# w_ple and the per-layer input brought and turned during the last product of the FFN, and its transposes one token ahead of its products

## The chip, the cores and the metric

One core of a Trainium2 chip runs the whole program. The metric is the device time of one execution in microseconds (us); the time of a kernel is the median of several runs. Engines are called TensorE (PE in the rows, its weight loads PEld), VectorE (DVE), ScalarE (ACT), GpSimd (POOL) and SyncE (SP, whose queue SPq issues most of the DMAs).

## The reference

The program computes one decoder layer for 1024 tokens of 1024 channels: two token mixers, a gated FFN, and at the end a gated per-layer input embedding, which is where the change lies. With `h` the sum after the mixers and `f` the FFN's inner activations (1024 tokens x 2816):

```
f = (gelu(f_gate) * f_val) @ w_down              # 2816 -> 1024
h = h + rmsnorm(f, norm_ffn_post)
e = (p @ w_ple) * sigmoid(h @ w_ple_gate)        # p: 1024 tokens x 256, w_ple: 256 x 1024
h = h + rmsnorm(e, norm_ple_post)                # the output
```

All is float32. A product in that precision is made of three matmuls (`mm3`, lines 342 to 347): each operand is split into a high part (a rounded copy, made by ScalarE) and a low part (the operand less the high part, made by VectorE or GpSimd), and high x high, high x low and low x high are summed in PSUM.

## The kernel before

**The down projection.** `down` (line 1426) makes `f @ w_down` by a scheme of seven block products in place of eight. The sums of activation blocks were written to DRAM before (`acts`), and four weight tiles `b11`, `b12`, `b21`, `b22` of 128 x 11 x 512 hold the blocks of w_down or differences of them. `product` (line 1446) is the loop of one block product: for each of 11 slices j, a pair of slices of `acts` is loaded into `araw` by SyncE every second j (a tag with two buffers); ScalarE makes the high halves of the activations (`whl`) and of the weights (`wdhl`, three buffers in the pool `wdT`); VectorE makes the low half of `whl`, GpSimd that of `wdhl` (all at line 313); TensorE makes 12 matmuls of 128 x 512 into four banks.

The last two products stand in `ple` (line 1504). The first of them, here called **P3**, multiplies the activations 5 with `b12`, which by then holds a difference of weights called **T3** here; the second, **P4**, multiplies the activations 2 with `b21`. Both tiles lie in the pool `wdB`. During P3 the eight blocks of w_ple_gate are loaded and split (`resident`, line 1300). During P4, at every third j, `res` (line 1515) closes one token block of the FFN: it squares it on ScalarE, and VectorE multiplies it with the norm's weights (line 1524) and adds the residual `h1r` (line 1527), with a small power on GpSimd between.

**The embedding.** After P4, `des.close()` gives up the pools of the weight tiles, and a pool `pleA` opens in their place. w_ple is loaded in two blocks of 128 x 1024 and split, the first low half on VectorE, the second on GpSimd. For each of eight blocks of 128 tokens, called tokens here, `inp` (line 1549) loads 128 x 256 of p, turns it by two transposes on TensorE and splits it while copying it out of PSUM (`to_T`, line 368: `ph` on ScalarE, `pl` on VectorE), and makes 12 matmuls into `pi`, which ScalarE copies to `pe` (four buffers). `turn` turns the finished h by eight transposes (`hh`, `hl`), and `out` makes the 48 matmuls of the gate (`pg`), the sigmoid, the norm and the store. The loop's round t makes turn(t+1), inp(t+3), res(t+4) and out(t); inp(0) to inp(2) stand ahead of it, so rounds 0 to 4 hold an input and rounds 5 to 7 none.

**What sets the order.** Buffers and waits are put in by the framework. The order on each engine is written ahead of time by a planner: it simulates the program with costs of its own, and each engine takes, of the instructions that are ready in the simulation, the one that stands first in the program. On the chip each engine then runs its list in that order, and an instruction that isn't ready holds up those behind it. `behind(a, b)` (line 1334) makes what is written in its block stand behind instruction a on a's engine and behind b on b's: `self.araw` is the last load of activations (SyncE), `up.lo` the last low half of activations (VectorE). It makes no wait.

Of the kernel before, what the change touches and what calls it, by code (L numbers as in the profile page):

```python
# [7 lines left out]
F32 = mybir.dt.float32  # L8
F32R = mybir.dt.float32r
# [6 lines left out]
P = 128  # L16
SEQ = 1024
NT = SEQ // P
DM = 1024
KD = DM // P  # L20
# [9 lines left out]
NF = DFF // P  # L30
# [264 lines left out]
class Body:  # L295
# [1130 lines left out]
    def down(self, hes, psd, bank, h1d, up):  # L1426

        nc, io = self.nc, self.io
        hf = NF // 2
        acts, wdn, pre = up.acts, up.wdn, up.pre  # L1430
        wes, des = ExitStack(), ExitStack()
        facc = self.pool(hes, "facc", side="right", own=True).tile([P, NT, DM], F32, name="facc")
        wA = self.pool(wes, "wdA", own=True)
        wB = self.pool(des, "wdB", side="right", own=True)
        thp = self.pool(des, "wdT", side="right", own=True)
        quad = {}
        for key, pool in (((0, 0), wA), ("T2", wA), ((1, 1), wA), ((1, 0), wB), ((0, 1), wB)):
            quad[key] = pool.tile([P, hf, 512], F32, name=f"wd{key[0]}{key[1]}")
        b11, b12, b21, b22, t2 = quad[0, 0], quad[0, 1], quad[1, 0], quad[1, 1], quad["T2"]

        def load_w(k, c, j0, j1):
            r = (k * hf + j0) * P
            nc.sync.dma_start(quad[k, c][:, j0:j1], wdn[r:r + (j1 - j0) * P, c * 512:c * 512 + 512].rearrange(
                "(j p) n -> p j n", p=P))

        def product(src, B, banks, first):

            for j in range(hf):
                if j % 2 == 0:
                    raw = self.wp.tile([P, 2, 512], F32, name="araw", tag="raw", bufs=2)  # L1450
                    m = min(2, hf - j)
                    self.araw = nc.sync.dma_start(raw[:, 0:m], acts[src, j:j + m].rearrange("j p n -> p j n")).ins
                a = up.ring(raw[:, j % 2], nc.vector)
                w = thp.tile([P, 2, 512], F32R, name="wdhl", tag="wdhl", bufs=3)
                self.wlo = self.hl(w[:, 0], w[:, 1], B(j) if callable(B) else B[:, j], nc.gpsimd)
                for t in range(4):
                    s = slice(t * P, t * P + P)
                    self.mm3(banks[t], a[:, 0, s], a[:, 1, s], w[:, 0], w[:, 1], first and j == 0, j == hf - 1,
                             not first)
                yield j  # L1460

        def run(gen, loads=()):

            loads = dict(loads)
            for j in gen:
                with self.behind(self.araw):
                    for ld in loads.get(j, ()):
                        load_w(*ld)

        c0, c1 = slice(0, 512), slice(512, DM)  # L1470
        npre = 2 * len(pre)
        Q = [bank("dq") for _ in range(4)]

        run(product(0, lambda j: pre[j // 2][:, j % 2] if j < npre else b11[:, j], Q, True),
            ((0, ((0, 0, npre, 8), (0, 0, 8, hf))), (2, ((1, 0, 0, 4),)), (4, ((1, 0, 4, 8),)), (6, ((1, 0, 8, hf),)),
             (8, ((1, 1, 0, 4),))))
        for t in range(4):
            nc.scalar.activation(facc[:, t, c0], Q[t], AF.Copy)
        M = [bank("dm") for _ in range(4)]
        run(product(1, b21, M, True), ((0, ((1, 1, 4, 8),)), (2, ((1, 1, 8, hf),)), (4, ((0, 1, 0, 4),)),  # L1480
                                       (6, ((0, 1, 4, 8),)), (8, ((0, 1, 8, hf),))))
        for t in range(4):
            nc.vector.tensor_add(facc[:, t, c0], M[t], facc[:, t, c0])
        Z = [bank("dz") for _ in range(4)]
        for j in product(6, b22, Z, True):
            with self.behind(up.lo):
                nc.vector.tensor_sub(b11[:, j], b12[:, j], pre[j // 2][:, j % 2] if j < npre else b11[:, j])
                nc.vector.tensor_sub(t2[:, j], b22[:, j], b11[:, j])
        for t in range(4):
            nc.scalar.activation(facc[:, t, c1], Z[t], AF.Copy)  # L1490
        for j in product(4, t2, Q, False):
            with self.behind(up.lo):
                nc.vector.tensor_sub(b12[:, j], b22[:, j], b12[:, j])
                nc.vector.tensor_sub(b21[:, j], b21[:, j], t2[:, j])
        for t in range(4):
            nc.scalar.activation(facc[:, 4 + t, c0], Q[t], AF.Copy)
        run(product(3, b11, Q, False))
        for t in range(4):
            nc.vector.tensor_add(facc[:, t, c1], Q[t], facc[:, t, c1])
            nc.scalar.activation(facc[:, 4 + t, c1], Q[t], AF.Copy)  # L1500
        wes.close()
        self.ple(hes, up, product, b12, b21, des, facc, psd, bank, h1d)

    def ple(self, hes, up, product, b12, b21, des, facc, psd, bank, h1d):

        nc, io = self.nc, self.io
        es = ExitStack()
# [5 lines left out]
        c0, c1 = slice(0, 512), slice(512, DM)  # L1513

        def res(t):

            h1 = [self.wq.tile([P, 512], F32, name="h1r", tag=f"s{t % 2 * 2 + i + 1}") for i in range(2)]
            for i, c in enumerate((c0, c1)):
                nc.sync.dma_start(h1[i], h1d[t, :, c])
            jk = self.wq.tile([P, DM], mybir.dt.bfloat16, name="jk", tag="p1", bufs=2)  # L1520
            f = facc[:, t]
            ss = self.small.tile([P, 1], F32, name="ss_h2", tag="ss", bufs=3)
            nc.scalar.activation(jk, f, AF.Square, accum_out=ss)
            nc.vector.tensor_mul(f, f, wf)
            r = self.rstd_of(ss, 1, 1.0 / DM, "h2")
            for i, c in enumerate((c0, c1)):
                nc.vector.scalar_tensor_tensor(f[:, c], f[:, c], r, h1[i], ALU.mult, ALU.add)

        N = [[bank("dn") for _ in range(4)] for _ in range(2)]
# [5 lines left out]
        for t in range(4):  # L1535
            nc.vector.tensor_add(facc[:, 4 + t, c1], N[0][t], facc[:, 4 + t, c1])
            nc.vector.tensor_add(facc[:, 4 + t, c0], N[0][t], facc[:, 4 + t, c0])
        for j in product(2, b21, N[1], True):
            if j % 3 == 0:
                with self.behind(self.araw, up.lo):  # L1540
                    res(j // 3)
        for t in range(4):
            nc.vector.tensor_add(facc[:, 4 + t, c0], N[1][t], facc[:, 4 + t, c0])
        des.close()
        pa = self.pool(es, "pleA", side="right", own=True)
        we = self.resident(pa, "w_ple", range(2))
        pes, hs = {}, {}

        def inp(t):

            pt = self.wp.tile([P, 256], F32, name="pt", tag="hi", bufs=2)
            nc.sync.dma_start(pt, io["p"][0, 0, t * P:t * P + P, :])
            ph = pa.tile([P, 2, P], F32R, name="ph", tag="ph", bufs=2)
            pl = pa.tile([P, 2, P], F32R, name="pl", tag="pl", bufs=2)
            self.to_T(pt, ph, pl, 0, psd, f"p{t}", kt=2, tag="d")
            pe = pes[t] = pa.tile([P, DM], F32, name="pe", tag="pe", bufs=4)
            for hf in range(2):
                c = slice(hf * 512, hf * 512 + 512)
                ps = bank("pi")
                for k, (wh, wl) in enumerate(we):  # L1560
                    self.mm3(ps, ph[:, k], pl[:, k], wh[:, c], wl[:, c], k == 0, k == 1)
                nc.scalar.activation(pe[:, c], ps, AF.Copy)

        def turn(t):
            hh = pa.tile([P, KD, P], F32R, name="hh", tag="hh", bufs=2)
            hl = pa.tile([P, KD, P], F32R, name="hl", tag="hl", bufs=2)
            self.to_T(facc[:, t], hh, hl, 0, psd, f"h{t}", tag="d")
            hs[t] = hh, hl

        def out(t):  # L1570
            hh, hl = hs.pop(t)
# [16 lines left out]
            for hf, c in enumerate(cs if t == NT - 1 else [slice(0, DM)]):  # L1588
                nc.vector.scalar_tensor_tensor(e[:, c], e[:, c], r0[:, 1:2], facc[:, t, c], ALU.mult, ALU.add)
                (nc.scalar, nc.sync)[hf].dma_start(self.out[0, t * P:t * P + P, c], e[:, c])  # L1590

        turn(0)
        for t in range(3):
            inp(t)
        for t in range(NT):
            if t + 1 < NT:
                turn(t + 1)
            if t + 3 < NT:
                inp(t + 3)
            if t + 4 < NT:  # L1600
                res(t + 4)
            out(t)
        es.close()
        hes.close()

# [22 lines left out]
```

## Time and profile before

| | |
|---|---|
| median of three runs | 1985.65 us (1981.07 to 1990.55) |
| the profiled execution's own time | 1987.6 us |
| its span, first to last instruction | 1985.9 us |
| TensorE busy | 1856.9 us (94%) |
| VectorE busy | 1237.1 us (62%) |
| ScalarE busy | 921.9 us (46%) |
| GpSimd busy | 703.1 us (35%) |
| mean granted clock of TensorE | 0.971 |

Busy time of TensorE is that of its matmuls, whose ends are modelled: two that follow each other at full rate overlap in the rows, so the pitch from start to start tells the rate. A wait is shown in brackets behind an instruction, with the instruction that ended it. Times in the rows are us from the span's start; P3 runs to about 1812, P4 from there to 1847, and the rest is the embedding.

### The profile page before, as it was taken

Reading aid. Unit: us, or ns where it says so; the run is one execution under the profiler, and the core shown is the slowest. Engines: PE = TensorE matmul, PEld = TensorE weight load, DVE = VectorE, ACT = ScalarE, POOL = GpSimd, SP = SyncE. Lnnn points to the kernel's source line nnn. Section 1 sums busy time; section 2 is a strip of 40 time slices with the busy share of each in tenths; the row PEclk is TensorE's granted clock in tenths of the full one; section 3 lists DMA queues with packets and bytes.
Section 4 is the critical chain, followed back from the end, with each engine's and each line's share of the span. In section 5 each row is a group of like instructions: output and inputs, shape, how many; then the busy total and the mean of one; then the engine's idle time right before and its main releaser. Section 6 shows DMA issues by size and latency. Waiting matters only on the chain. (4 is left out here: it accounts for less than half of the span.)

```text
span 1985.9 us, 25905 instructions
## 1 busy us (share of the span) xinstructions
PE 1856.9 (94%) x9247; PEld 1535.3 (77%) x9247; DVE 1237.1 (62%) x2364; ACT 921.9 (46%) x1818; POOL 703.1 (35%) x538
## 2 busy tenths in 40 slices
PE   7999989999989999999999959999999999999898
PEld 6788778888778888778777847787787877777776
DVE  5437933341367667776783497776676864958543
ACT  4344222232367667776662334444444544455332
POOL 2132112223122112231162056666666664545100
PEclk9998999999989999999999979999999999999999
DMA  5124333322311010110063212232323356245201
GB/s 163 33 78 116 93 86 90 84 84 80 99 32 33 27 38 29 42 59 22 22 233 129 86 63 91 90 101 85 122 83 109 100 186 239 75 155 173 88 35 43
DMA packets 182943, 178.68 MB, mean 90 GB/s; under 512 B 27869, under 2 KB 133662, under 8 KB 182814
## 3 DMA queue, kind: packets, MB, share of 16 engines
q1 hardware_dynamic: 180592, 170.33, 27.7%
q10 hardware_dynamic: 2222, 6.69, 0.9%
q8 instruction: 73, 1.20, 0.3%
q14 instruction: 56, 0.46, 0.1%
HBM read 132.65 MB, written 44.34 MB: 89 GB/s over the span
## 5 line engine op out<-in xcount | busy, mean ns | idle before, releaser
L345 PE MATMUL pj<-uh,whi 128*128 128x512 f32 x640 | 263.0, 411 | 8.8 <-DVE y L515 6.6
L346 PE MATMUL pj<-ul,whi 128*128 128x512 f32 x640 | 258.4, 404 | 0.0
L347 PE MATMUL pj<-uh,wlo 128*128 128x512 f32 x640 | 258.3, 404 | 0.0
L313 POOL TENSOR_TENSOR wlo<-raw,whi 128x1024 fp32r<-128x1024 f32 x48 | 116.8, 2435 | 323.5 <-ACT whi L324 287.7
L345 PEld LDWEIGHTS pj<-uh,whi 128*128 128x128 f32 x640 | 123.5, 193 | 36.4 <-issue 5.7
L313 POOL TENSOR_TENSOR whl<-s,whl 128x512 fp32r<-128x512 f32 x88 | 126.8, 1448 | 60.2 <-ACT whl L1331 60.2
L347 PEld LDWEIGHTS pj<-uh,wlo 128*128 128x128 f32 x640 | 123.1, 192 | 29.0
L346 PEld LDWEIGHTS pj<-ul,whi 128*128 128x128 f32 x640 | 123.4, 193 | 25.9
L313 POOL TENSOR_TENSOR wdhl<-wd,wdhl 128x512 fp32r<-128x512 f32 x66 | 97.9, 1495 | 78.4 <-ACT wdhl L1331 76.9
L313 POOL TENSOR_TENSOR whl<-raw,whl 128x512 fp32r<-128x512 f32 x66 | 105.4, 1599 | 49.2 <-ACT whl L1331 48.7
L313 DVE TENSOR_TENSOR whl<-araw,whl 128x512 fp32r<-128x512 f32 x77 | 87.1, 1141 | 56.2 <-ACT whl L1331 55.0
L1243 DVE TENSOR_TENSOR Tl<-pt,Th 128x512 fp32r<-128x512 f32 (+1 forms) x152 | 92.6, 617 | 24.9 <-ACT Th L1242 21.2
L345 PE MATMUL q<-mxh,whl 128*128 128x512 f32 x264 | 104.5, 399 | 3.3 <-ACT u L106 2.1
L1213 ACT ACTIVATE Pt<-Pt,nm 128x640 f32<-128x640 f32 (+7 forms) x128 | 93.0, 728 | 30.1 <-DVE nm L1211 29.7
L346 PE MATMUL q<-mxl,whl 128*128 128x512 f32 x264 | 104.2, 395 | 0.0
L347 PE MATMUL q<-mxh,whl 128*128 128x512 f32 x264 | 103.5, 395 | 0.2 <-POOL whl L313 0.2
L1242 ACT ACTIVATE Th<-pt 128x512 fp32r<-128x512 f32 (+1 forms) x152 | 79.2, 538 | 50.0 <-PE po L1246 32.5
L324 ACT ACTIVATE whi<-raw 128x1024 fp32r<-128x1024 f32 x48 | 50.5, 1052 | 83.7 <-PE pj L346 55.8
L1239 PE MATMUL pt<-ident,Pt 128*128 128x128 f32 x528 | 82.9, 277 | 2.8 <-DVE Tl L1243 1.3
L126 DVE SCALAR_TENSOR_TENSOR yg<-c,cv,yg 128x1 f32<-128x1 f32 (+2 forms) x88 | 81.4, 929 | 0.9 <-ACT yg L123 0.9
L1331 ACT ACTIVATE whl<-s 128x512 fp32r<-128x512 f32 x88 | 54.7, 624 | 56.9 <-PE n L347 44.1
L1205 PE MATMUL ps<-kst,qs 128*128 128x512 f32 (+3 forms) x192 | 70.4, 368 | 6.7 <-DVE mx L1208 4.9
(534 smaller groups left out, 5142.0 us busy)
## 6 DMA issues: line engine op xcount, KB each, us to landing
raw<-in_w_up SPq DMA_DIRECT2D x44, 512.0 KB
raw<-in_w_in SPq DMA_DIRECT2D x40, 512.0 KB
araw<-acts SPq DMA_DIRECT2D x35, 512.0 KB
acts<-sd SPq DMA_DIRECT2D x44, 256.0 KB
gates_d<-yz SPq DMA_DIRECT2D x40, 256.0 KB
acts<-yv SPq DMA_DIRECT2D x33, 256.0 KB
gt<-gates_d SPq DMA_DIRECT2D x32, 256.0 KB
wd<-in_w_down SPq DMA_DIRECT2D x7, 1024.0 KB
```

The lines of the kernel that those rows point to most:

```text
L126: self.body.nc.vector.scalar_tensor_tensor(y, src, w, y, ALU.mult, ALU.add)
L313: return eng.tensor_sub(lo, src, hi.bitcast(F32)).ins
L324: nc.scalar.activation(hi, raw, AF.Copy)
L345: nc.tensor.matmul(ps, lh, rh, start=start, stop=False, skip_group_check=more)
L346: nc.tensor.matmul(ps, lh, rl, start=False, stop=False, skip_group_check=more)
L347: nc.tensor.matmul(ps, ll, rh, start=False, stop=stop, skip_group_check=more)
L1205: nc.tensor.matmul(ps[:, 0:n], qs[:, hh], kh, start=True, stop=False)
L1213: nc.scalar.activation(Pt[:, hh, 0:nk], Pt[:, hh, 0:nk], AF.Exp, scale=2.0 ** -(h0 + hh + 1), bias=nm[:, br, hh:hh + 1], accum_out=rs[:, b ...
L1239: nc.tensor.transpose(pt[:, b, hh], Pt[:, hh, (b0 + b) * P:(b0 + b + 1) * P], self.ident)
L1242: nc.scalar.activation(Th[:, 0:m], pt[:, 0:m], AF.Copy)
L1243: nc.vector.tensor_sub(Tl[:, 0:m], pt[:, 0:m], Th[:, 0:m].bitcast(F32))
L1331: self.nc.scalar.activation(hi, src, AF.Copy)
```

## The change

The pool `pleA` goes. The tile of T3 (tag `wd01`) is taken over after P3 as one flat tile `cB`, which holds the four halves of w_ple and two slots of turned input; the tile `b21` (tag `wd10`) is taken over after P4 as `cH`, for the turned h; `pe` takes the three buffers of `wdhl`. Within P4, both blocks of w_ple are loaded and split at j = 1 and 2, both low halves on VectorE; p is loaded in two loads of 512 KB (four tokens each) at j = 4 and 5; tokens 0 and 1 are turned at j = 8 and 10. The raw data go through the two buffers `rawv` that the gate's blocks used in P3. Behind P4, `inp_T` makes the transposes of a token and `inp` its products: round t now makes turn(t+1), inp_T(t+3), inp(t+2), res(t+4), out(t). The work computed is the same.

```diff
-        for j in product(2, b21, N[1], True):
-            if j % 3 == 0:
-                with self.behind(self.araw, up.lo):
-                    res(j // 3)
-        for t in range(4):
-            nc.vector.tensor_add(facc[:, 4 + t, c0], N[1][t], facc[:, 4 + t, c0])
-        des.close()
-        pa = self.pool(es, "pleA", side="right", own=True)
-        we = self.resident(pa, "w_ple", range(2))
-        pes, hs = {}, {}
+
+        flat = lambda tag: wB.tile([P, NF // 2 * 512], F32R, name="ple" + tag, tag=tag)
+        cB = flat("wd01")
+        we, raws, pes, hs = [], [], {}, {}
+        cut = lambda t, i, n, w: t[:, i * n:i * n + n].rearrange("p (k w) -> p k w", w=w)
+
+        def w_ple(k):
+            raw = self.wq.tile([P, DM], F32, name="raw", tag="rawv", bufs=2)
+            nc.sync.dma_start(raw, self.dram2d("w_ple", 2 * P, DM)[k * P:k * P + P, :])
+            w = [cB[:, (2 * k + i) * DM:(2 * k + i + 1) * DM] for i in range(2)]
+            self.hl(*w, raw, nc.vector)
+            we.append(w)
+
+        def p_in(n):
+            raw = self.wq.tile([P, 4, 256], F32, name="pt", tag="rawv", bufs=2)
+            nc.sync.dma_start(raw, io["p"][0, 0, n * 512:n * 512 + 512, :].rearrange("(t p) n -> p t n", p=P))
+            raws.append(raw)
+
+        def inp_T(t):
+
+            o = 4 * DM // 256 + t % 2 * 2
+            self.to_T(raws[t // 4][:, t % 4], cut(cB, o, 256, P), cut(cB, o + 1, 256, P), 0, psd, f"p{t}", kt=2, tag="d")
 
         def inp(t):
 
-            pt = self.wp.tile([P, 256], F32, name="pt", tag="hi", bufs=2)
-            nc.sync.dma_start(pt, io["p"][0, 0, t * P:t * P + P, :])
-            ph = pa.tile([P, 2, P], F32R, name="ph", tag="ph", bufs=2)
-            pl = pa.tile([P, 2, P], F32R, name="pl", tag="pl", bufs=2)
-            self.to_T(pt, ph, pl, 0, psd, f"p{t}", kt=2, tag="d")
-            pe = pes[t] = pa.tile([P, DM], F32, name="pe", tag="pe", bufs=4)
+            o = 4 * DM // 256 + t % 2 * 2
+            ph, pl = cut(cB, o, 256, P), cut(cB, o + 1, 256, P)
+            pe = pes[t] = thp.tile([P, DM], F32, name="pe", tag="wdhl", bufs=3)
...
+        also = {1: (w_ple, 0), 2: (w_ple, 1), 4: (p_in, 0), 5: (p_in, 1), 8: (inp_T, 0), 10: (inp_T, 1)}
+        for j in product(2, b21, N[1], True):
+            with self.behind(self.araw, up.lo):
+                if j % 3 == 0:
+                    res(j // 3)
+                if j in also:
+                    also[j][0](also[j][1])
+        for t in range(4):
+            nc.vector.tensor_add(facc[:, 4 + t, c0], N[1][t], facc[:, 4 + t, c0])
+        cH = flat("wd10")
+
         def turn(t):
-            hh = pa.tile([P, KD, P], F32R, name="hh", tag="hh", bufs=2)
-            hl = pa.tile([P, KD, P], F32R, name="hl", tag="hl", bufs=2)
-            self.to_T(facc[:, t], hh, hl, 0, psd, f"h{t}", tag="d")
-            hs[t] = hh, hl
+            hs[t] = [cut(cH, t % 2 * 2 + i, DM, P) for i in range(2)]
+            self.to_T(facc[:, t], *hs[t], 0, psd, f"h{t}", tag="d")
...
         turn(0)
-        for t in range(3):
-            inp(t)
+        inp(0)
+        inp_T(2)
+        inp(1)
         for t in range(NT):
             if t + 1 < NT:
                 turn(t + 1)
             if t + 3 < NT:
-                inp(t + 3)
+                inp_T(t + 3)
+            if t + 2 < NT:
+                inp(t + 2)
             if t + 4 < NT:
                 res(t + 4)
             out(t)
+        des.close()
         es.close()
```

## Rows read from the trace of the kernel before

**Rows 1.** The page's head.
```profile
span 1985.9 us, 25905 instructions
```

**Rows 2.** Busy time by stretch: length, five engines, granted clock, DMA share, GB/s.
```profile
1812.20:1847.10 34.90, 32.69 (x140) 25.02 (x139) 31.49 (x35) 11.46 (x20) 18.01 (x14) 1.00 0.45 147
1847.10:1861.50 14.40, 10.14 (x45) 7.72 (x44) 9.00 (x12) 6.81 (x14) 3.80 (x2) 0.88 0.25 78
...
1942.50:1954.60 12.10, 12.10 (x59) 9.86 (x58) 5.29 (x9) 3.51 (x8) 0.55 (x1) 1.00 0.11 43
```

**Rows 3.** TensorE's waits, 1780 to 1986: total us, times, longest.
```profile
PE pi L345 <- ACT ph L376: 7.1, 6, 3.3
PE dn L347 <- DVE whl L313: 2.1, 3, 0.9
```

**Rows 4.** Chain of work that ended last, seam behind P4: start, us, what.
```profile
1843.72 5.48 DMA raw<-in_w_ple
...
1849.28 1.06 ACT w_pleh L1310
...
1851.31 0.28 ACT ph L376
```

**Rows 5.** Timeline of TensorE, seam: start, us, what, [idle before <-releaser].
```profile
1846.92 0.49 PE L374 MATMUL pT_h<-ident,facc 128*128 128x128 f32 x3
1847.93 0.44 PE L374 MATMUL pT_p<-ident,pt 128*128 128x128 f32 x2 [0.51 <-DMA pt<-in_p]
1851.64 0.50 PE L345 MATMUL pi<-w_pleh,ph 128*128 128x512 f32 x1 [3.27 <-ACT ph L376]
...
1853.75 0.80 PE L345 MATMUL pi<-w_pleh,ph 128*128 128x512 f32 x1 [0.47 <-ACT ph L376]
...
1855.63 0.62 PE L374 MATMUL pT_p<-ident,pt 128*128 128x128 f32 x2
...
1856.31 0.40 PE L345 MATMUL pi<-w_pleh,ph 128*128 128x512 f32 x1
```

**Rows 6.** Timeline of TensorE, one round of the token loop.
```profile
1877.55 1.03 PE L374 MATMUL pT_h<-ident,facc 128*128 128x128 f32 x8
1878.42 0.38 PE L374 MATMUL pT_p<-ident,pt 128*128 128x128 f32 x2
1879.66 0.50 PE L345 MATMUL pi<-w_pleh,ph 128*128 128x512 f32 x1 [0.85 <-ACT ph L376]
...
1893.77 1.03 PE L374 MATMUL pT_h<-ident,facc 128*128 128x128 f32 x8
```

**Rows 7.** Timeline of TensorE, two slices of P3.
```profile
1806.60 1.10 PE L345 MATMUL dn<-wdhl,whl 128*128 128x512 f32 x4
...
1809.41 1.10 PE L345 MATMUL dn<-wdhl,whl 128*128 128x512 f32 x4
```

**Rows 8.** VectorE's groups by shape, 1781.2 to 1812.2: busy us, mean ns.
```profile
L313 DVE TENSOR_TENSOR w_ple_gatel<-raw,w_ple_gateh 128x1024 fp32r<-128x1024 f32 x7 | 9.6, 1377 | 2.5 <-ACT w_ple_gateh L1310 2.3
```

**Rows 9.** Timeline of VectorE, P3, P4 and the seam.
```profile
1794.56 2.32 DVE L313 TENSOR_TENSOR w_ple_gatel<-raw,w_ple_gateh 128x1024 fp32r<-128x1024 f32 x1
...
1814.99 3.48 DVE L313 TENSOR_TENSOR whl<-araw,whl 128x512 fp32r<-128x512 f32 x2
...
1823.17 0.68 DVE L313 TENSOR_TENSOR whl<-araw,whl 128x512 fp32r<-128x512 f32 x1
...
1842.73 0.68 DVE L313 TENSOR_TENSOR whl<-araw,whl 128x512 fp32r<-128x512 f32 x1
1845.49 2.48 DVE L1543 TENSOR_TENSOR facc<-dn,facc 128x512 f32<-128x512 f32 x4 [2.08 <-PE dn L347]
...
1858.30 0.42 DVE L377 TENSOR_TENSOR pl<-pT_p,ph 128x256 fp32r<-128x256 f32 x1 [2.18 <-ACT ph L376]
```

**Rows 10.** Timeline of SyncE's queue, P4.
```profile
1816.80 7.45 SPq L1452 DMA_DIRECT2D araw<-acts  x2
```

**Rows 11.** Timeline of GpSimd, P4.
```profile
1811.51 6.40 POOL L313 TENSOR_TENSOR wdhl<-wd,wdhl 128x512 fp32r<-128x512 f32 x4
```

More of the change, by code (lines that the diff above doesn't have):

```diff
@@ L1437, in down @@
         for key, pool in (((0, 0), wA), ("T2", wA), ((1, 1), wA), ((1, 0), wB), ((0, 1), wB)):
-            quad[key] = pool.tile([P, hf, 512], F32, name=f"wd{key[0]}{key[1]}")
+            quad[key] = pool.tile([P, hf, 512], F32, name=f"wd{key[0]}{key[1]}", tag=f"wd{key[0]}{key[1]}")
         b11, b12, b21, b22, t2 = quad[0, 0], quad[0, 1], quad[1, 0], quad[1, 1], quad["T2"]
@@ L1501, in down, with ple @@
         wes.close()
-        self.ple(hes, up, product, b12, b21, des, facc, psd, bank, h1d)
-    def ple(self, hes, up, product, b12, b21, des, facc, psd, bank, h1d):
+        self.ple(hes, up, product, b12, b21, des, wB, thp, facc, psd, bank, h1d)
+    def ple(self, hes, up, product, b12, b21, des, wB, thp, facc, psd, bank, h1d):
         nc, io = self.nc, self.io
```

## The prediction

> **What bounds the kernel now.** I read the views in this order: span, busy time by stage, TensorE's waits at the end, the chain of waits, then the order on each engine there. The span is 1985.9 us and TensorE works through nearly all of it [rows 1], so a change is worth what it gives TensorE back where TensorE stands still. The diff touches the part behind about 1805 us: the product P4 (1812.2 to 1847.1), the seam behind it, and eight tokens of the per-layer embedding.
>
> In P4 TensorE is busy 32.69 of 34.90 us, and VectorE 31.49; in the seam, 1847.1 to 1861.5, TensorE works 10.14 of 14.40 us, and the granted clock has a mean of 0.88 [rows 2]. The reader is to see two different causes there. In P4 the waits, 2.1 us in three, are for `whl`, VectorE's low halves; behind P4 they are 7.1 us in six for `ph`, the turned layer input [rows 3]. What ended last in the seam is a load: `w_ple` takes 5.48 us from issue to landing, ScalarE then copies it (1.06), and behind that copy stands ph (0.28) for the first input product [rows 4].
>
> **What the waits cost.** A product matmul is issued every 0.234 us (12 in 2.81 us [rows 7]), a transpose every 0.109 (8 in 0.87 us [rows 6]).
> The seam: from 1846.92, where P4's products have been issued, to 1856.31, where full pitch is back, are 9.39 us [rows 5]. Nine product matmuls and nine transposes lie in it: 9 x 0.234 + 9 x 0.109 = 3.09. Lost: 6.3 us. That is the waits of 0.51, 3.27 and 0.47 [rows 5], about 1.1 us of matmuls at half the rate (the four from 1853.75 to 1855.63 stand 0.47 apart; the lower of the two clock levels, 1.2 GHz, after TensorE had stood), and the restarts.
> The token loop: with an input in it a round takes 16.22 us (1877.55 to 1893.77 [rows 6]). Its work is 48 + 12 products and 8 + 2 transposes, 60 x 0.234 + 10 x 0.109 = 15.13. Lost: 1.09, of which 0.85 is the wait for ph, which comes straight behind the transposes that ph is copied from [rows 6]. There are four such rounds: 4.4 us. A round without an input took 12.10 and has no loss [rows 2] (48 x 0.234 + 0.87 = 12.10), so this is all there is to win in the loop.
> Together 10.7 us.
>
> **The change part by part.**
> *w_ple (two 512 KB loads, two copies, two subtractions) goes into P4.* Its place is the tile of T3, read for the last time in P3, so it need not wait for P4. The cover for the loads is P4's 34.9 us. Gone is the 3.27 us wait; late next at that place is `hh` of token 0 or the bank of the first `pi`, and both are at hand, since turn(0)'s place is the tile that P4's last copy frees. Cost: the copies lie on ScalarE, which is busy only 11.46 us in P4 [rows 2]. The low halves lie on VectorE, which has hardly a gap there: TensorE's three waits in P4 are already waits for VectorE, and what is queued ahead of a `whl` moves TensorE. The nearest rows are the gate's low halves, same shape and engine, mean 1.377 us of seven in P3, and 2.32 for the longest [rows 8, 9]. I take 2 x 1.38 = 2.8 us, all on the path.
> *The input in two loads of 512 KB in the place of eight of 128 KB, queued in P4 behind P4's own loads; two of the eight turnings in P4.* SyncE's queue is in order: `p_in` waits for a buffer that w_ple's low half frees, and behind it stands the next `araw`. In P4 SyncE holds two araw triggers over 7.45 us because the buffers are not free [rows 10], so there is room for p_in if VectorE has finished w_ple by then; I cost it at nothing, and at one exposed load (below) if not. Four transposes move from behind the seam into P4, no gain or loss, with 0.1 us for each of two changes from products to transposes and back. Their two `pl` subtractions (0.42 us each [rows 9]) come late in P4: VectorE's last whl ends at 1843.41 and it then stands 2.08 us [rows 9], which covers 0.84.
> *Transposes one token ahead in the loop.* The matmuls that cover the copy are the previous input's 12 (2.8 us) and the 48 of the gate (11.2 us); a copy of some 0.3 us needs neither in full. Late next would be `pe`: three buffers in place of four, but also made two rounds ahead in place of three, so its slot was and is freed by the token just finished. I cost it at nothing.
> *What stays lost.* 0.1 us at each of five changes between transposes and products, so the gain is 10.7 - 0.5 = 10.2 us, rounded to 10.1.
>
> Sum: 10.1 - 2.8 - 0.2 = 7.1 us less. P4's cost is the uncertain term. Its low end is below nothing: a new order on VectorE can also take away the three waits (-2.1 [rows 3]). Its high end is two low halves of 2.32, two pl and the changes: 4.64 + 0.84 + 0.2 = 5.7. I take 3.0, near the mean of the gate's rows, since these are the same instruction under the same neighbours. The gain is then 12.2 to 4.4.
>
> Whether two subtractions cost their mean or the long form hangs on GpSimd: a `whl` takes 0.68 us at 1823.17, but two take 3.48 from 1814.99 on, while GpSimd makes four `wdhl` in 6.40 [rows 9, 11]. The Trainium skill, "SBUF — State Buffer", section "Who interferes with whom", has a rule that speaks against the change: a VectorE instruction with two SBUF inputs and a GpSimd instruction that reads SBUF exclude each other, the later one standing still for the whole of the first. The trace agrees (0.68 against 1.74). By that rule both low halves would meet `wdhl` work and cost 2.32 each, and the time would be 1980.4, inside the forecast's own range; by the rows' mean it is the sum above.
>
> The profiled execution took 1987.6 us (1.7 outside its span), 1.95 above the median of the three shown, 1985.65. The sum gives 1980.5 against the profiled time, and 1978.5 against the median, which I forecast.
>
> **The rivals.**
> *B, P4 takes the work for nothing.* VectorE has waits of its own in P4, before TensorE frees the last sums (2.08 [rows 9]) among them, and the low halves could fall into such gaps. For it: the planner fills gaps. Against: the low halves are traced early in P4 and the 2.08 us lie at its end. Gain 10.1 to 12.2: 1975.6 to 1973.4.
> *C, the loop doesn't change.* The transposes are ahead, but the product waits for another thing, `pe`'s slot or a bank, as long as before. For it: ScalarE makes ph, hh, pe, sigmoid and squares in one queue. Against: the rounds without input lose nothing [rows 2]. The loop's 4.0 us stay: 1982.5.
> *D, one exposed load.* p_in stands on SyncE's queue ahead of an araw, or ScalarE's copy of w_ple is ordered ahead of whl and its load is late. One landing of 5.48 us [rows 4] comes onto the path, with 1.1 us of lower clock behind it: 1985.1.
> *E, slower.* The same mechanism at its worst: each of the four loads put into P4 is waited for by an engine that P4 needs (ScalarE for the two of w_ple, SyncE and TensorE, whose transposes stand in line between P4's products, for the two of p). Price 4 x 5.48 + 1.1 = 23.0 us, 1978.5 + 23.0 = 2001.5. It decides from the second exposed load on: 2 x 5.48 is more than the 7.1 won. For it: TensorE's line is fixed by a model of when a load lands, and where w_ple lands late today the queue behind it did wait. Against: P3 carries eight such gate loads beside its own without one wait of TensorE [rows 3] (none of the 2.1 us lies there).
>
> **How the numbers follow.** Forecast A (P4 costs 1 to 5.7 us; own range 1976 to 1981.5) has 0.54, B 0.20, C 0.08, D 0.11, E 0.07. 0.5% is 9.9 us, about what a measurement of this kernel tells from no change. Only B passes it, with the scatter of runs (1981.07 to 1990.55) around A's fast end: A, C, D and B's slow edge are no change. Faster 0.25, same 0.68, slower 0.07. The range holds A, C and D and most of B, with the scatter: 1973 to 1987.
>
> **What would show it.** Right: no wait of `pi` for `ph` in the loop, rounds of about 15.2 us in place of 16.22; the seam without a wait over 0.5 us and without the lower clock; P4 longer by 1 to 5 us, its waits again for `whl`, with a w_ple low half just ahead of the late one on VectorE. Wrong: a P4 as short as before (B), rounds over 16 (C), TensorE or ScalarE waiting in P4 for `raw` of w_ple, `pt` or `araw` (D, E).

## The result, and the profile after

The changed kernel takes 1975.38 us (median of 18 runs, 1968.77 to 1983.15) against 1985.88 (18 runs) before: ratio 0.9947, interval 0.9936 to 0.9959, 10.5 us less. The forecast was 1978.5 with 7.1 us to win. A second set of runs on another occasion gave 0.9930 (0.9914 to 0.9946).

The profiled execution took 1981.25 us. Its earlier part ran long: P3 begins at 1786.2 in it and at 1781.3 in the one of before, although the program is the same up to there. So the two are compared from P3's first product to the last product of the gate: 196.4 us before, 185.0 after, 11.4 us less. In the trace of the second set the same stretch takes 186.4 us, 10.0 less.

First the stretches (columns as in [rows 2]): P4, the seam and a round of the loop.

```profile
1817.10:1851.60 34.50, 32.96 (x142) 25.48 (x141) 32.32 (x40) 14.11 (x25) 19.56 (x14) 1.00 0.52 176
1851.60:1866.00 14.40, 14.40 (x73) 11.91 (x72) 6.37 (x12) 7.55 (x14) 0.55 (x1) 1.00 0.11 37
1872.70:1887.80 15.10, 15.10 (x71) 12.31 (x70) 8.21 (x15) 6.02 (x13) 1.10 (x2) 1.00 0.20 71
```

Against [rows 2]: behind P4 TensorE now works 14.40 of 14.40 us, not 10.14, with the clock at 1.00, not 0.88. P4 is no longer than before, although VectorE, ScalarE, GpSimd and the DMAs are busier in it.

TensorE's waits in P4 after the change; behind P4 there are none (columns as in [rows 3]):

```profile
PE dn L346 <- POOL wdhl L313: 0.8, 2, 0.6
PE dn L347 <- DVE whl L313: 0.6, 1, 0.6
```

The 7.1 us of waits for `ph` of [rows 3] are gone, and of the 2.1 for `whl` one of 0.6 is left, with two short ones for GpSimd. The seam and a round on TensorE's timeline (as in [rows 5, 6]):

```profile
1851.51 0.60 PE L374 MATMUL pT_h<-ident,facc 128*128 128x128 f32 x4
1851.87 0.48 PE L345 MATMUL pi<-plewd 128*128 128x512 f32 x1
...
1872.76 1.03 PE L374 MATMUL pT_h<-ident,facc 128*128 128x128 f32 x8
1873.63 0.38 PE L374 MATMUL pT_p<-ident,pt 128*128 128x128 f32 x2
1873.77 0.48 PE L345 MATMUL pi<-plewd 128*128 128x512 f32 x1
...
1887.83 1.03 PE L374 MATMUL pT_h<-ident,facc 128*128 128x128 f32 x8
```

(`plewd` is the new tile: w_ple, ph and pl in one name.) The first input product stands 0.36 us behind the end of P4's products, where it stood 4.7 [rows 5]; a round takes 15.07 us, not 16.22 [rows 6], and `pi` follows its transposes without a wait, since these belong to the next token.

### The profile page after: what moved, and what is told of

Same layout as the page of the kernel before. It is cut to its first block, busy times and chain, and to the rows that moved or that the text cites. A ratio compares the mean times of both kernels' runs of the same rounds, so it can differ in the third digit from the quotient of the medians.

```text
span 1979.5 us, 25890 instructions
## 1 busy us (share of the span) xinstructions
PE 1856.0 (94%) x9247; PEld 1537.6 (78%) x9247; DVE 1235.3 (62%) x2365; ACT 921.9 (47%) x1818; POOL 702.0 (35%) x537
## 5 line engine op out<-in xcount | busy, mean ns | idle before, releaser
L345 PEld LDWEIGHTS pj<-uh,whi 128*128 128x128 f32 x640 | 123.7, 193 | 34.6 <-issue 4.4
L313 POOL TENSOR_TENSOR whl<-s,whl 128x512 fp32r<-128x512 f32 x88 | 126.4, 1444 | 59.0 <-ACT whl L1331 59.0
L1205 PE MATMUL ps<-kst,qs 128*128 128x512 f32 (+3 forms) x192 | 70.4, 369 | 6.7 <-DVE mx L1208 4.9
```

The costliest lines, as they stand in the source:

```text
L313: return eng.tensor_sub(lo, src, hi.bitcast(F32)).ins
L345: nc.tensor.matmul(ps, lh, rh, start=start, stop=False, skip_group_check=more)
L1205: nc.tensor.matmul(ps[:, 0:n], qs[:, hh], kh, start=True, stop=False)
```

## The experiments

Two measures are used. The ratio is over whole runs, with its interval. The stretches are read from each kernel's trace, one execution each: P4 begins 132 products of 0.2345 us behind P3's first one and ends with its own last product; "behind" runs from there to the end of the gate's last product. P4 holds 5 transposes in some kernels and 8 or 12 in others (0.11 us each), so the sum of the two is the safer column.

| kernel | P4 | behind | sum | ratio to before (interval) |
|---|---|---|---|---|
| before | 34.7 | 130.8 | 165.5 | 1 |
| changed | 34.4 | 119.6 | 154.0 | 0.9947 (0.9936 to 0.9959) |
| changed, again | 35.8 | 119.6 | 155.5 | 0.9930 (0.9914 to 0.9946) |
| e1, loop only | 34.6 | 125.8 | 160.4 | 0.9976 (0.9962 to 0.9991) |
| e2, P4 part only | 34.2 | 126.4 | 160.6 | 0.9966 (0.9949 to 0.9983) |
| e3, low halves twice | 36.4 | 119.0 | 155.3 | 0.9931 (0.9906 to 0.9957) |
| e5, no low halves on VectorE | 35.8 | 119.2 | 155.0 | 0.9925 (0.9903 to 0.9946) |
| e4, low halves on GpSimd | 38.7 | 118.7 | 157.4 | 0.9954 (0.9937 to 0.9972) |
| e7, P4's wdhl on VectorE | 36.0 | 118.1 | 154.1 | 0.9941 (0.9926 to 0.9955) |
| e6, b21 later | 34.0 | 119.6 | 153.6 | 0.9912 (0.9896 to 0.9929) |
| e6, again | 34.1 | 119.6 | 153.8 | 0.9910 (0.9889 to 0.9931) |
| e8, e6 and four products' wdhl on VectorE | 33.3 | 118.0 | 151.4 | 0.9895 (0.9876 to 0.9913) |

### The two halves of the change, each alone

e1 leaves w_ple and p behind P4 as before, and only parts transposes and products of a token:

```diff
-        for t in range(3):
-            inp(t)
+        inp_T(0)
+        inp_T(1)
+        inp(0)
+        inp_T(2)
+        inp(1)
         for t in range(NT):
...
             if t + 3 < NT:
-                inp(t + 3)
+                inp_T(t + 3)
+            if t + 2 < NT:
+                inp(t + 2)
```

> Only the loop part of the change: w_ple and p are loaded behind P4 as before, but each token's transposes stand one token ahead of its products. Theory N (the parts add up: seam 6.3 us, loop 4.4 us, P4 costs nothing): the four waits of 0.85 us go, rounds take about 15.1 us, the seam still stands for w_ple's load; 4.4 us less than before, ratio 0.9978. Rival R (the rounds' waits only moved because the seam was gone and the queue behind it ran early): waits stay, ratio 1.000.

e2 is the changed kernel with the transposes put back straight ahead of their products:

```diff
-        inp_T(2)
         inp(1)
         for t in range(NT):
...
-            if t + 3 < NT:
-                inp_T(t + 3)
             if t + 2 < NT:
+                inp_T(t + 2)
                 inp(t + 2)
```

> Only the P4 part of the change: w_ple and p come during P4, tokens 0 and 1 are turned there, but from token 2 on the transposes stand straight ahead of the products of the same token. Theory N: the seam's 6.3 us go, P4 stays at about 34.4 us, and six rounds lose about 1.05 us each (6.3, against 4.4 before): 1985.9 - 6.3 - 0.9 + 1.9 = 1980.6, ratio 0.9973. Rival R (the seam carries the whole gain): ratio 0.995.

TensorE's waits from P4 on, in e1:

```profile
PE dn L347 <- DVE whl L313: 2.1, 3, 0.9
PE pi L345 <- ACT ph L376: 1.6, 1, 1.6
PE pT_p L374 <- DMA pt<-in_p: 1.2, 1, 1.2
PE pT_h L374 <- DVE hl L377: 0.5, 1, 0.5
```

and in e2:

```profile
PE pi L345 <- ACT plewd L376: 5.1, 6, 0.9
PE dn L347 <- DVE whl L313: 1.0, 1, 1.0
PE dn L346 <- POOL wdhl L313: 0.6, 2, 0.4
```

e1 keeps P4's three waits to the tenth of a us (its P4 is that of before), still stands 3.3 us in three waits at the seam, and has none in the rounds behind it: 5.0 us less behind P4. e2 has no wait at the seam, and one in each of six rounds, two more than before. Behind P4 it wins 4.4 us; with the two added waits of 1.13 us (16.2 less 15.07) that is 6.7 for the seam. Theory N holds: the ratios, 0.9976 and 0.9966, lie beside the 0.9978 and 0.9973 expected, and the parts add up. e1's rival falls by its interval and its rounds. e2's rival, 0.995, lies inside e2's interval; what speaks against it is the six waits in e2's rounds and what e1 wins without the seam. 6.7 us for the seam and four rounds of 1.13 make the 11.2 us that the changed kernel wins behind P4; e1's 5.0 are its four rounds and half a us of the seam.

### What w_ple's low halves cost in P4

This is the term that the forecast put at 2.8 us. e3 makes each low half twice; e5 takes them from VectorE and leaves out the low part of w_ple (a copy of the weight stands there). The comments name the run.

```diff
             self.hl(*w, raw, nc.vector)
+            self.lo_of(w[1], raw, w[0], nc.vector)     # e3
...
-            self.hl(*w, raw, nc.vector)                # e5
+            nc.scalar.activation(w[0], raw, AF.Copy)
+            nc.scalar.activation(w[1], raw, AF.Copy)
```

> The changed kernel, but VectorE makes each of the two low halves of w_ple twice, 2 x 1.21 us more work of the kind whose price the forecast put on the path. Theory N (VectorE has room in P4, the low halves fill waits and move other work away from GpSimd): P4 34.4 to 35.4 us, ratio 0.9947 to 0.9953. Rival V (the forecast's: VectorE is full and each low half moves the end of P4 by its length): P4 at 36.8 or more, ratio 0.996.

> The changed kernel, but the low halves of w_ple are plain copies made by ScalarE in place of VectorE's subtractions, so the low part of that weight is left out of the computation (a copy of the weight stands there). Theory N: P4 within 0.7 us of the changed kernel's 34.4, ratio 0.9947. Rival V: P4 shorter by the 2.4 us that VectorE is freed of, about 32.0, ratio 0.9935.

Neither theory had it. With twice the work P4 and what follows take 155.3 us, with none of it 155.0, and the changed kernel's two traces, of one and the same program, 154.0 and 155.5. So neither doubling the work nor taking it away moves the time by more than the scatter of one program, and no price by length is seen. In e5 VectorE, freed of that work, took longer for its whl, 1210 ns in place of the changed kernel's 891:

```profile
L313 DVE TENSOR_TENSOR whl<-araw,whl 128x512 fp32r<-128x512 f32 x10 | 11.9, 1210 | 0.9 <-ACT whl L1331 0.9
```

But neither run is a clean test, for in both TensorE stands for something else. Its timeline in e3 and in e5:

```profile
1826.42 0.66 PE L374 MATMUL pT_p<-ident,pt 128*128 128x128 f32 x4 [2.12 <-DMA pt<-in_p]
```

```profile
1816.87 0.63 PE L374 MATMUL pT_p<-ident,pt 128*128 128x128 f32 x4 [1.89 <-DMA pt<-in_p]
```

In these two P4 has not one wait for whl; it waits once for p, about 2 us, and the granted clock of P4 falls to 0.95 in both. Whether a whl would have been late had TensorE not stood for p can't be read from them. The causes differ. In e5 the planner put the four transposes of p behind 28 of P4's 132 products, where the changed kernel has them behind 40 and 44: too early for the load. In e3 they stand where the changed kernel has them, behind 44, and the load is late (its trigger is shown below). Both are rival D of the forecast in a form in which TensorE does the waiting: the wait is smaller than the 5.48 us priced there, since the load is only exposed in part. In the changed kernel p has landed when its transposes come.

e4 puts the low halves on GpSimd:

```diff
-            self.hl(*w, raw, nc.vector)
+            self.hl(*w, raw, nc.gpsimd)
```

> The changed kernel with both low halves of w_ple on GpSimd in place of VectorE. Theory O (what P4 costs hangs on the order of the lists and on p's landing, not on the length of the low halves): P4 within 1.5 us of 34.4, with or without a wait for p; ratio 0.992 to 0.996. Rival S (VectorE's price is its collisions with GpSimd): two more GpSimd instructions of some 2.4 us hold up two or more VectorE instructions by about 1.1 us each, whl waits come back, P4 36 us or more.

P4 takes 38.7 us, 4.3 more (0.4 of it four transposes), so theory O fails by size, though its cause is there. S has the size, and its cause is there on VectorE, whose whl take longer than the 891 ns of the changed kernel (shown further down); but TensorE doesn't wait for one. TensorE in e4, and VectorE's whl in its P4:

```profile
1813.20 0.50 PE L346 MATMUL dn<-wdhl,whl 128*128 128x512 f32 x1 [0.97 <-POOL wdhl L313]
1819.31 0.63 PE L374 MATMUL pT_p<-ident,pt 128*128 128x128 f32 x4 [2.72 <-DMA pt<-in_p]
```

```profile
L313 DVE TENSOR_TENSOR whl<-araw,whl 128x512 fp32r<-128x512 f32 x10 | 12.4, 1251 | 1.2 <-ACT whl L1331 1.0
```

The load's trigger shows on SyncE's queue, here that of the changed kernel, of e4 and of e3:

```profile
1820.45 0.37 SPq L1452 DMA_DIRECT2D araw<-acts  x1
1821.58 5.70 SPq L1553 DMA_DIRECT2D pt<-in_p  x2
```

```profile
1813.72 0.37 SPq L1452 DMA_DIRECT2D araw<-acts  x1
1814.20 2.15 SPq L1553 DMA_DIRECT2D pt<-in_p  x2
```

```profile
1817.25 0.37 SPq L1452 DMA_DIRECT2D araw<-acts  x1
1822.56 0.38 SPq L1554 DMA_DIRECT2D pt<-in_p  x1
```

In e4 it follows at once the araw that it is queued behind, and TensorE gets going 5.1 us later, about a landing: there, as in e5, the transposes stand behind 28 products, too early. In e3 it comes 5.3 us behind its araw, and 1.1 in the changed kernel, because its buffer still holds a block of w_ple whose low half is being made a second time. So e3's added work does cost time, but, as far as its trace shows, through the buffer that p's load lands in and not through a late whl. A wdhl made late behind GpSimd's two longer subtractions costs e4 another 0.97 us.

### What fills VectorE in P4: GpSimd beside it

Two traces of the changed kernel, with the same lists, differ by 1.4 us in P4. The first, on VectorE, GpSimd and TensorE:

```profile
1825.67 1.21 DVE L313 TENSOR_TENSOR plewd<-raw,plewd 128x1024 fp32r<-128x1024 f32 x1
...
1828.00 0.67 DVE L313 TENSOR_TENSOR whl<-araw,whl 128x512 fp32r<-128x512 f32 x1
```

```profile
1825.69 2.34 POOL L313 TENSOR_TENSOR wdhl<-wd,wdhl 128x512 fp32r<-128x512 f32 x1 [1.18 <-ACT wdhl L1331]
```

```profile
1828.73 1.20 PE L347 MATMUL dn<-wdhl,whl 128*128 128x512 f32 x4 [0.63 <-DVE whl L313]
```

and the second, taken beside e4, e6 and e7, with GpSimd:

> The changed kernel once more, beside the next three on the same chip: ratio 0.9947 again, and a second trace of the same order. All theories: P4 34.4 us, from P3's start to the last product 185.0 us; the spread between the two traces is what the others are measured against.

```profile
1814.89 2.21 DVE L313 TENSOR_TENSOR plewd<-raw,plewd 128x1024 fp32r<-128x1024 f32 x1
...
1818.22 0.68 DVE L313 TENSOR_TENSOR whl<-araw,whl 128x512 fp32r<-128x512 f32 x1
```

```profile
1818.95 1.20 PE L347 MATMUL dn<-wdhl,whl 128*128 128x512 f32 x4 [1.95 <-DVE whl L313]
```

```profile
1814.72 1.30 POOL L313 TENSOR_TENSOR wdhl<-wd,wdhl 128x512 fp32r<-128x512 f32 x1 [1.00 <-ACT wdhl L1331]
```

In both the low half meets a `wdhl` of GpSimd. In the first the two start within 0.02 us of each other; the low half keeps its 1.21 us, and GpSimd's instruction takes 2.34. In the second the wdhl starts 0.17 us ahead: it keeps 1.30 us, and the low half takes 2.21. It had also started 0.5 us later in P4, so the whl behind it is 1.5 us later, and TensorE waits 1.95 us for it, not 0.63. Here the forecast's mechanism is at work, a low half ahead of the late whl, but what it costs is decided by which of the two instructions starts first. e2 and the two traces of e6 have the same lists in P4, and go as the first: there the low half takes 1.21 us, the wdhl 2.31 to 2.35, and P4 34.0 to 34.2. e7 takes GpSimd's reading out of P4:

```diff
-        def product(src, B, banks, first):
+        def product(src, B, banks, first, eng=nc.gpsimd):
...
-                self.wlo = self.hl(w[:, 0], w[:, 1], B(j) if callable(B) else B[:, j], nc.gpsimd)
+                self.wlo = self.hl(w[:, 0], w[:, 1], B(j) if callable(B) else B[:, j], eng)
...
-        for j in product(2, b21, N[1], True):
+        for j in product(2, b21, N[1], True, nc.vector):
```

> The changed kernel with the low halves of P4's weights (wdhl, 11 of 128x512) on VectorE in place of GpSimd. Theory S (an instruction of VectorE that meets one of GpSimd takes 1.1 us more, and that is most of what fills VectorE in P4): whl falls to 0.68 us and L1527 to 0.74 throughout, VectorE's busy time in P4 rises by no more than 2 us over 32.2 although 7.5 us of work are added, and P4 stays within 1 us of 34.4. Rival F (VectorE is simply full): busy time reaches the whole of P4, and P4 grows by 5 us or more.

VectorE's groups in P4 (busy us, mean ns), before:

```profile
L1527 DVE SCALAR_TENSOR_TENSOR facc<-facc,rb_h,h1r 128x512 f32<-128x512 f32 x8 | 12.9, 1649 | 2.0 <-POOL rb_h L355 2.0
L313 DVE TENSOR_TENSOR whl<-araw,whl 128x512 fp32r<-128x512 f32 x10 | 9.8, 1009 | 0.0
```

changed:

```profile
L1527 DVE SCALAR_TENSOR_TENSOR facc<-facc,rb_h,h1r 128x512 f32<-128x512 f32 x8 | 11.8, 1515 | 2.2 <-POOL rb_h L355 2.2
L313 DVE TENSOR_TENSOR whl<-araw,whl 128x512 fp32r<-128x512 f32 x10 | 8.8, 891 | 0.6 <-ACT whl L1331 0.6
...
L313 DVE TENSOR_TENSOR plewd<-raw,plewd 128x1024 fp32r<-128x1024 f32 x2 | 2.4, 1210 | 0.0
L1581 DVE TENSOR_TENSOR facc<-dn,facc 128x512 f32<-128x512 f32 x3 | 1.9, 676 | 0.0
```

and e7:

```profile
L313 DVE TENSOR_TENSOR whl<-araw,whl 128x512 fp32r<-128x512 f32 x10 | 6.8, 682 | 0.0
L313 DVE TENSOR_TENSOR wdhl<-wd,wdhl 128x512 fp32r<-128x512 f32 x10 | 6.8, 682 | 0.0
L1527 DVE SCALAR_TENSOR_TENSOR facc<-facc,rb_h,h1r 128x512 f32<-128x512 f32 x8 | 5.7, 749 | 1.1 <-POOL rb_h L355 0.9
```

The reader is to see three things. In the changed kernel's first trace the added 2.4 us of low halves are nearly paid by what two other groups lose, 12.9 - 11.8 + 9.8 - 8.8 = 2.1 us: a new order, in which VectorE stands less for GpSimd. The 2.08 us for which VectorE stood before the last sums [rows 9] are gone too (the last row). And in e7 VectorE takes over 6.8 us of work in this window and is busy 31.0 us in all, less than the changed kernel's 32.3. F falls, and S holds in what it says of VectorE; its P4, within 1 us of 34.4, was missed: P4 takes 36.0 us (0.4 of it four more transposes). P4 with what follows is 154.1 us, so e7 wins nothing yet, since its new order lets TensorE wait twice, 2.0 us in all, for VectorE's sums of P3.

### The same reading one stage earlier

In the product with T2 (activations 4) VectorE also has no gap, and at its end TensorE stands 3.0 us. e6 moves one of the two subtractions that each slice adds there to the next product:

```diff
         for j in product(4, t2, Q, False):
             with self.behind(up.lo):
                 nc.vector.tensor_sub(b12[:, j], b22[:, j], b12[:, j])
-                nc.vector.tensor_sub(b21[:, j], b21[:, j], t2[:, j])
...
-        run(product(3, b11, Q, False))
+        for j in product(3, b11, Q, False):
+            with self.behind(up.lo):
+                nc.vector.tensor_sub(b21[:, j], b21[:, j], t2[:, j])
```

> The changed kernel with the 11 subtractions that update b21 moved from the product with T2, where VectorE has no gap, into the product behind it. The same reading one stage earlier: TensorE stands 3.0 us there for the copies of the sums, which wait behind a whl whose araw waits for VectorE, and runs 14 matmuls at the lower clock behind it. Theory Q (VectorE's list is what is late there): the 3.0 us wait and the lower clock go, 4 to 6 us less than the changed kernel, ratio to the kernel before 0.9920. Rival L (the wait is for araw's landing whatever VectorE does): 0 to 1 us less, ratio 0.9945.

> The kernel with b21's update moved once more, on the chip of the run beside it. Theory Q: ratio 0.9912 again and no wait of TensorE for the copies of the sums; rival L: back to the changed kernel's 0.9935 to 0.9947.

TensorE's waits in the two products, changed kernel, and then e6:

```profile
PE dq L345 <- ACT facc L1496: 3.0, 1, 3.0
PE dq L347 <- DVE whl L313: 0.7, 1, 0.7
PE dq L346 <- POOL wdhl L313: 0.2, 1, 0.2
```

```profile
PE dq L346 <- POOL wdhl L313: 0.2, 1, 0.2
```

The wait is gone, and the stretch from the last matmul of the product before to P3's start is 62.9 and 62.8 us in the two traces of e6, against 66.7 to 70.4 in nine traces of kernels with the old order there. In five of these nine the granted clock falls behind the wait (to a mean of 0.95 to 0.98 over the stretch), and they take 69.3 to 70.4; the four at full clock take 66.7 to 67.9, so e6 wins 3.8 to 5.1 us there even against those. Theory Q holds. Over whole runs e6's interval lies clear of the changed kernel's first one and overlaps the second.

e8 is e6 with e7's edit in the last four products (activations 4, 3, 5 and 2):

> The kernel with b21's update moved, and with the low halves of the weights (wdhl) on VectorE in the last four products instead of GpSimd. Theory S (the work of VectorE is cheap where GpSimd reads nothing beside it): no 1.77 us forms of 128x512 are left in these products, VectorE is no busier than with GpSimd's help, and TensorE's waits there go under 2 us in all; 0 to 3 us less than with b21's update moved alone, ratio to the kernel before 0.990 to 0.9915. Rival F (four products are too much for VectorE alone): waits for whl and wdhl return, ratio 0.993 or more.

VectorE's groups over the four products, and TensorE's only wait from there to the end:

```profile
L313 DVE TENSOR_TENSOR whl<-araw,whl 128x512 fp32r<-128x512 f32 x46 | 31.5, 684 | 1.0 <-ACT whl L1331 1.0
L313 DVE TENSOR_TENSOR wdhl<-wd,wdhl 128x512 fp32r<-128x512 f32 x33 | 22.7, 687 | 13.7 <-ACT wdhl L1331 13.4
```

```profile
PE dq L346 <- DVE wdhl L313: 0.7, 1, 0.7
```

No long form is left (a whl has a mean of 0.68 us in e8 and 1.12 in e6 over these products). P4 and what follows take 151.4 us, 14.1 less than before and 2.3 less than e6. Theory S holds (its ratio passed by 0.0005) and F falls: over the four products VectorE is busy 100.6 us, in e6 108.2. The median is 1964.31 us, ratio 0.9895: its interval is clear of the kernel before, and just clear of the changed kernel's two. That it beats e6 rests on the stretch of one trace, with the stretch ahead of P3 0.5 us longer (63.3 us); the intervals overlap.

## Why the prediction was right or wrong

The time lies in the range, and the sign is right; but the range was wide enough for four of the five cases, so this says little. The size was short by 3.4 us, and the likeliest case was not the one that came: by its time and the first trace's P4 it was rival B, to which the forecast gave 0.20 (the second trace's P4, 1.2 us longer than before, is at A's low edge). B's reason, that the low halves fall into VectorE's waits, is seen in part (the 2.08 us before the last sums are gone); the rest is that VectorE stands less for GpSimd in the new order, which is near what the forecast named as its own low end.

- *The seam, 6.3 us.* Right: 6.7 by e2. What was named as late next (hh, a bank) was not late.
- *The loop, 4.4 us.* Right: 4 x 1.13 = 4.5 us; the rounds lose nothing now, 15.07 us against the 15.13 of the sum.
- *What stays lost, 0.5 us.* Wrong by its size, as the seam and the rounds run without a loss to speak of. Seam and loop together were put at 10.1 and gave 11.2, of which 0.3 are three transposes more that P4 now takes.
- *P4, "2 x 1.38 = 2.8 us, all on the path".* This is the step that failed. P4 changed by -0.3 us in one trace and +1.2 in another, those transposes included. The argument went from "VectorE has no gap" to "each us added is a us on the path". The runs showed that some 10 of the 31.5 us that fill VectorE in P4 are time in which it stands for GpSimd: with GpSimd's low halves out (e7) it does 7 us more work and is less busy. So a low half costs what its place in the list makes of it: about nothing where it starts ahead of the wdhl that it meets (four traces of this order), a us or so where it comes behind it, just ahead of a late whl (one trace). Doubling or removing the work (e3, e5) gave no clean price, since both runs also exposed p's load.
- *The rule weighed.* The Trainium skill, "SBUF — State Buffer", section "Who interferes with whom", was weighed as a reason for a higher price. The rule stands: e7 and e8 show it plainly (1.65 us falls to 0.75, and 1.12 to 0.68), and so do the two traces of the changed kernel, in which the later of two instructions took 1.0 us longer. What the forecast made too little of is that it works both ways: a new order can also take meetings away, and where VectorE comes first it is GpSimd that stands.
- *p's loads at nothing, or one exposed landing (D).* Right for the changed kernel, and its mechanism is real: 1.9 to 2.7 us in e3, e4 and e5, all of them with an edit that does not touch p's load. e3 is the forecast's own case, VectorE not done with w_ple when p_in wants the buffer.
- *E and C.* Neither was seen. No trace has two exposed loads.

Open: why the planner puts p's transposes behind 28 products in e4, e5, e7 and e8 and behind 40 to 44 in the changed kernel, e2, e3 and e6; that the edit shifts its simulated times is likely and wasn't tested. So is how often P4 falls out long with the changed kernel's order: it did in one of five traces.

## What to carry to other kernels

Before pricing work on a full engine, look at the spread of one form's durations on it: where the same instruction takes 0.68 us and 1.78, the engine may be partly waiting for a neighbour, as here, and then the lever is the neighbour, not the amount of work. A wait that is read as a gap between two rows of one engine can be summed with confidence, as the seam and the rounds were; a cost on a list that will be ordered anew deserves a wide bound on both sides of nothing. And a load moved ahead is only as early as the buffer it lands in, and whoever stands in line for it pays if the planner trusted its landing.

## What the runs showed of the hardware

VectorE's subtraction of 128x512 takes 0.68 us alone and up to 1.78 beside GpSimd's (the changed kernel's first trace). Where two of them met in the changed kernel's two traces, the one that started first kept its time (1.21 and 1.30 us) and the other took 1.0 us longer (2.34 and 2.21); executions of the same lists differed in which came first. In P4 of the kernel before the two groups named above took 22.7 us, and at e7's means would have taken 12.8, so, by this estimate, some 10 us of VectorE's 31.5 [rows 2] were such standing. With eleven of GpSimd's subtractions added to its own (e7), VectorE was busy 31.0 us in place of 32.3 and 33.7 (the two traces of the changed kernel). One and the same program takes 1968.8 to 1983.2 us, and a good part of that arises long before the part that was changed: P3 began at 1786.2 in one trace of the changed kernel and at 1774.9 in the other.
